# Sixteen input row tiles placed k times 32 bytes behind multiples of 512 bytes, in a kernel with three matmuls per weight block

## The chip, the cores and the metric

The kernel runs on one core of one Trainium2 chip. The metric is the device time of one execution in microseconds (us); the time before is the median of three runs. Profiled times count from the start of the span. PE is the matrix engine (TensorE), PEld its weight loads, ACT the scalar engine, DVE the vector engine, POOL GpSimd and SP the engine whose queue issues nearly all transfers.

## What is computed

The reference is a stack of layers over one sequence of 256 tokens of width 2048, in float32: a mixer (stick-breaking attention beside a gated delta rule), cross attention to a memory of 256 rows, a convolutional feed-forward layer of inner width 5632, an attention with forget gates and one with a sliding window. Nearly all of the work is in products of the activations with 11 weight matrices:

```python
proj = h @ w_in[l]                                   # 2048 x 7184
x = x + mixed @ w_out[l]                             # 2048 x 2048
x = x + memory_cross_attention(rmsnorm(x, xattn_norm[l]), mem_n, w_xq[l], w_xkv[l], w_xo[l])
u = causal_dwconv(h @ w_up, conv_w) + conv_b         # 2048 x 11264
x = x + (jax.nn.silu(gate) * up) @ w_down            # 5632 x 2048
p = h @ fox_w_in[j];  x = x + y @ w_out              # 2048 x 8224, 2048 x 2048
p = h @ swa_w_in[j];  x = x + y @ w_out              # 2048 x 4608, 2048 x 2048
```

## The kernel before

**Data.** Activations lie transposed: XT has 16 row tiles of 128 features by 256 tokens. A row tile that goes into a product is split into two parts that add up to it (`split`, L207): a rounded part in float32r, written by ACT, and the remainder, written by DVE. Both lie in one tile of 2 x 256 elements (2048 bytes in each partition): `xh` for the 16 scaled row tiles of the residual stream (pool `xp`, 16 buffers, made by `new_x` and `fox_x`), and `mv`, `mix` and `mm` for inner activations, in pools of their own. `xh` is written anew in five places (before w_in, w_xq, w_up, the forget-gate layer, the sliding-window layer), each time for k = 0 to 15 in order, so that row tile k always has buffer k.

**Weights.** Weights come from HBM in granules of up to KG = 8 row blocks of 128 x 256 (`granules`, L239): 1 MB each, in `wt`, NWT = 3 buffers. The first product of the kernel begins with smaller granules. Each granule is turned into float32r in chunks of up to KC = 4 row blocks: ACT copies the chunk to `wh` (L258), DVE subtracts it from `wt` to give the remainder `wl` (L259, listed as L147). `wh` and `wl` have NWC = 4 buffers each, of 4096 bytes in a partition. After each chunk `tick` lets the side work (attention heads, norms) go on by a step.

**Matmuls.** For each row block and each half of 128 columns, `linB` issues three matmuls of 128 x 256 into one accumulation: `wh` times the rounded part, `wh` times the remainder, `wl` times the rounded part. The weight block is the stationary operand, and each matmul loads it anew. `linA` swaps the roles: the row tile is stationary and the weights move. All are issued by `mm`, which is why the profile shows them under L136.

**Addresses.** In the built program `wh` and `wl` buffers begin 384 bytes behind a multiple of 512, and so does every block in them, since blocks are 512 or 1024 bytes apart. The `xh` tiles begin at 384 too, the `mv`, `mix` and `mm` tiles at 128.

**Order.** A scheduler orders the instructions of each engine by the dependences of tiles and by when buffers come free; each queue then runs its instructions in that order. A `wt` buffer is free again when DVE has made the last `wl` of its granule; that is what an SP transfer of weights waits for.

Of the kernel before, what the change touches and what calls it, by code (L numbers as in the profile page):

```python
# [10 lines left out]
F32R = mybir.dt.float32r  # L11
# [4 lines left out]

S, D, P = 256, 2048, 128
KT = D // P
KG, KC = 8, 4
NWT, NWC = 3, 4  # L20

WIDTH = {"norm": 1, "mem": 1, "gdn": 1, "sb": 1, "xa": 2, "at": 2}
NEG = -1e30
# [99 lines left out]
def body(ctx: ExitStack, tc: tile.TileContext, d: dict, out: bass.AP, stop=None):  # L123
# [6 lines left out]
    xp = Lined(ctx.enter_context(tc.tile_pool(name="xp", bufs=16)))  # L130
# [38 lines left out]
    def V(name):  # L169
        o, n = COLS[name]  # L170
        return cols[:, o : o + n]
# [35 lines left out]
    def split(mv, src, scale=None):  # L207

        if scale is None:
            act(mv[:, 0, :], src, AF.Copy)  # L210
            tt(mv[:, 1, :], src, mv[:, 0, :].bitcast(F32), ALU.subtract)
        else:
            act(mv[:, 0, :], src, AF.Copy, scale=scale)  # L213
            stt(mv[:, 1, :], src, scale, mv[:, 0, :].bitcast(F32), ALU.mult, ALU.subtract)
# [129 lines left out]
    def column(r):  # L344
# [10 lines left out]
        later("norm", work())  # L355
        return c

    def new_x(k, g):
        mv = xp.tile([P, 2, 256], F32R, tag="xh", name="xh")
        split(mv, XT[:, k, :], V(g)[:, k : k + 1])  # L360
        return mv

# [13 lines left out]
    def then(norm, g):  # L376
        xs = []

        def after(k):
            xs.append(new_x(k, g))  # L380
            norm.add(XT[:, k, :])

        return xs, after
# [27 lines left out]
    def first_x(k):  # L411
        n = 2 if k < 4 else 4
        if k % n == 0 and k not in made:
            src = d["xT"][k * P : (k + n) * P, :].rearrange("(k p) s -> p k s", p=P)
            nc.sync.dma_start(XT[:, k : k + n, :], src)
        if k not in made:
            made[k] = new_x(k, "mix_norm")
        return made[k]

    xh = [lambda k=k: first_x(k) for k in range(KT)]  # L420
# [343 lines left out]
    xh, after = then(norm, "xattn_norm")  # L764
# [10 lines left out]
    def new_mv():  # L775
        return mvbox[0].tile([P, 2, 256], F32R, tag="mv", name="mv")
# [25 lines left out]
    with tc.tile_pool(name="xa", bufs=2) as xa_:  # L802
# [61 lines left out]
        xh, after = then(norm, "ffn_norm")  # L864
# [15 lines left out]
    fx = []  # L880

    def fox_x(k):
        mv = xp.tile([P, 2, 256], F32R, tag="xh", name="xh")
        split(mv, XT[:, k, :], fg[:, k : k + 1])
        fx.append(mv)
        norm.add(XT[:, k, :])
        norm2.add(XT[:, k, :], V("final_norm")[:, k : k + 1])

    cw, cb = V("ffn_conv"), V("ffn_conv_bias")
    with tc.tile_pool(name="ff", bufs=2) as ff_:  # L890
# [15 lines left out]
        for n in range(22):  # L906
# [6 lines left out]
            for j in range(2):  # L913
                mv = new_mv()
# [9 lines left out]
    xh = fx  # L924
# [176 lines left out]
    for gidx in range(8):  # L1101
        c0 = 256 * gidx
        q = ap_.tile([P, 2, 256], F32, tag="qk", name="q")
        k = ap_.tile([P, 2, 256], F32, tag="qk", name="k")
# [24 lines left out]
    xh, after = then(norm, "norm_g_2b")  # L1129
# [103 lines left out]
def build(arrays, stop=None):  # L1233
    import concourse.bacc as bacc

    nc = bacc.Bacc("TRN2", target_bir_lowering=False, num_devices=1)
    d = {n: nc.dram_tensor(f"in_{n}", a.shape, F32, kind="ExternalInput").ap() for n, a in arrays.items()}
    out = nc.dram_tensor("out_0", (D, S), F32, kind="ExternalOutput").ap()
    with tile.TileContext(nc) as tc:
        body(tc, d, out, stop)  # L1240
    return nc
# [9 lines left out]
```

## Time and profile before

| | before |
|---|---|
| median of 3 runs | 2270.25 us (2270.0 to 2272.79) |
| the profiled execution | 2270.89 us |
| its span, first to last instruction | 2269.1 us |
| PE busy in the span | 2248.3 us (99%) |
| PEld busy | 2208.0 us (97%) |
| DVE, ACT, POOL busy | 1500.1, 1203.9, 119.0 us |
| matmuls that read an `xh` tile | 11,904 of 19,214 |
| moved from HBM | 375.66 MB, 166 GB/s over the span |

Between the span and the time of the same execution lie 1.8 us. Matmuls are pipelined: one that is listed with 283 ns overlaps the two behind it, so the distance from start to start is what counts, not the duration.

### The profile page before, as it was taken

To read this page: it belongs to the slowest core of one execution; us is meant where nothing else is said; L and a number is where in the kernel's file an instruction comes from. 1 tells how busy PE (TensorE), PEld (TensorE's weight loads), DVE (VectorE), ACT (ScalarE), POOL (GpSimd) and SP (SyncE) were. 2 spreads that over 40 slices of the span, in tenths; PEclk is the share of its full clock that TensorE was granted. 3 is DMA by queue.
4 is the path that set the end of the run, shared out by engine and by line. 5 is a ranking of instruction groups with operands and counts; after the bars stand their busy time and mean duration, and the time that the engine had idled before them with its cause. 6 is when DMAs were issued, how large, how long until landed. Compare 5 with 4: busy or idle time off the path is not lost.

```text
span 2269.1 us, 45530 instructions
## 1 busy us (share of the span) xinstructions
PE 2248.3 (99%) x19214; PEld 2208.0 (97%) x19214; DVE 1500.1 (66%) x2474; ACT 1203.9 (53%) x2036; POOL 119.0 (5%) x161
## 2 busy tenths in 40 slices
PE   9999999999999999999999999999999999999997
PEld 9999999999999999999999999999999999999997
DVE  7756566467587756656765777766666666787864
ACT  6544545356565534544544556555555554566652
POOL 1101010000000000000000000000110000000011
PEclk9999999999999999999999999999999999999999
DMA  7433434345455565555556546444444455444443
GB/s 265 149 131 131 147 118 146 112 160 196 164 189 184 168 202 185 167 186 191 185 167 204 181 164 214 151 168 167 168 166 168 149 186 186 152 165 149 159 159 111
DMA packets 62350, 380.69 MB, mean 168 GB/s; under 512 B 6593, under 2 KB 12865, under 8 KB 19521
## 3 DMA queue, kind: packets, MB, share of 16 engines
q1 hardware_dynamic: 60768, 375.94, 49.4%
q8 instruction: 150, 2.46, 0.4%
q10 hardware_dynamic: 1232, 1.06, 0.1%
q0 software_dynamic: 144, 0.79, 0.1%
q14 instruction: 56, 0.45, 0.1%
HBM read 375.66 MB, written 2.10 MB: 166 GB/s over the span
## 4 chain that ended last, share of the span: by engine, by line
PE 94%; DVE 3%; ACT 2%; issue 1%; POOL 0%; DMA 0%; SPq 0%; DVEq 0%; ACTq 0%; POOLq 0%
PE linb L136 79%; PE lina L136 7%; PE zps L136 2%; PE yps L136 1%; PE ptps L976 1%; PE nps L136 1%; DVE wl L147 1%; PE wsp L136 1%; PE xps L136 1%; DVE y L150 0%; ACT wh L258 0%; PE snp L136 0%; PE mps L136 0%; POOL e L492 0%; DMA wt<-in_w_in 0%
## 5 line engine op out<-in xcount | busy, mean ns | idle before, releaser
L136 PE MATMUL linb<-xh,wh 128*128 128x256 f32 x7104 | 1300.7, 285 | 2.2 <-ACT xh L213 1.7
L258 ACT ACTIVATE wh<-wt 128x1024 fp32r<-128x1024 f32 (+2 forms) x713 | 744.8, 1047 | 890.4 <-PE linb L136 738.7
L147 DVE TENSOR_TENSOR wl<-wt,wh 128x1024 fp32r<-128x1024 f32 (+2 forms) x713 | 869.8, 1223 | 467.3 <-ACT wh L258 461.0
L136 PEld LDWEIGHTS linb<-xh,wh 128*128 128x128 f32 x7104 | 1108.4, 192 | 10.8 <-issue 4.7
L136 PE MATMUL linb<-xh,wl 128*128 128x256 f32 x3552 | 1005.9, 283 | 0.0
L136 PEld LDWEIGHTS linb<-xh,wl 128*128 128x128 f32 x3552 | 681.6, 192 | 0.1
L136 PE MATMUL linb<-mv,wh 128*128 128x256 f32 x2560 | 462.6, 283 | 0.0
L136 PEld LDWEIGHTS linb<-mv,wh 128*128 128x128 f32 x2560 | 399.3, 192 | 0.5 <-issue 0.3
L136 PE MATMUL linb<-mv,wl 128*128 128x256 f32 x1280 | 362.3, 283 | 0.0
L136 PEld LDWEIGHTS linb<-mv,wl 128*128 128x128 f32 x1280 | 245.5, 192 | 0.2 <-issue 0.2
L136 PE MATMUL lina<-wh,xh 128*128 128x256 f32 x832 | 157.9, 286 | 0.0
L136 PEld LDWEIGHTS lina<-wh,xh 128*128 128x128 f32 x832 | 132.0, 192 | 0.6 <-issue 0.3
L136 PE MATMUL lina<-wl,xh 128*128 128x256 f32 x416 | 117.9, 283 | 1.0 <-DVE wl L147 1.0
L150 DVE SCALAR_TENSOR_TENSOR y<-pre,cols,y 128x256 f32<-128x256 f32 x248 | 103.4, 480 | 0.3 <-ACT y L504 0.2
L136 PE MATMUL linb<-mix,wh 128*128 128x256 f32 x512 | 94.1, 285 | 0.2
L136 PEld LDWEIGHTS linb<-mix,wh 128*128 128x128 f32 x512 | 80.0, 192 | 1.2 <-issue 0.3
L136 PEld LDWEIGHTS lina<-wl,xh 128*128 128x128 f32 x416 | 79.7, 192 | 1.2 <-DVE wl L147 1.2
L136 PE MATMUL linb<-mix,wl 128*128 128x256 f32 x256 | 72.7, 284 | 0.3 <-DVE wl L147 0.3
L147 DVE TENSOR_TENSOR pre<-linb,rstd 128x512 f32<-128x512 f32 x56 | 38.7, 692 | 41.3 <-PE linb L136 41.2
L1028 POOL CAST kd<-kd 64x512 fp32r<-64x512 f32 x32 | 36.2, 1131 | 355.2 <-ACT kd L1025 353.8
L150 DVE SCALAR_TENSOR_TENSOR XT<-linb,XT 128x512 f32<-128x512 f32 x48 | 33.2, 692 | 29.1 <-PE linb L136 29.0
L895 POOL MEMSET pre<- 128x4 f32 x44 | 4.3, 102 | 879.0 <-ACT wh L258 673.6
(291 smaller groups left out, 1800.5 us busy)
## 6 DMA issues: line engine op xcount, KB each, us to landing
wt<-in_w_up SPq DMA_DIRECT2D x88, 1024.0 KB, 5.2
wt<-in_fox_w_in SPq DMA_DIRECT2D x64, 1024.0 KB, 5.1
wt<-in_w_in SPq DMA_DIRECT2D x53, 1024.0 KB, 5.1
wt<-in_swa_w_in SPq DMA_DIRECT2D x36, 1024.0 KB, 5.1
wt<-in_w_down SPq DMA_DIRECT2D x32, 1024.0 KB, 4.9
wt<-in_w_out SPq DMA_DIRECT2D x16, 1024.0 KB, 5.3
wt<-in_fox_w_out SPq DMA_DIRECT2D x16, 1024.0 KB, 5.1
wt<-in_swa_w_out SPq DMA_DIRECT2D x16, 1024.0 KB, 5.2
```

The source lines that it names most:

```text
L136: nc.tensor.matmul(o, lhsT, rhs, start=start, stop=stop, skip_group_check=True)
L147: vec.tensor_tensor(o, a, b, op=op)
L150: vec.scalar_tensor_tensor(o, a, s, b, op0=op0, op1=op1)
L258: act(wh[:], wt[:, h : h + n, :], AF.Copy)
L895: gps.memset(pre[:, :, 0:2], 0.0)
L976: nc.tensor.transpose(tps[:, b * P : b * P + P], p[:, b * P : b * P + P], ident)
L1028: gps.tensor_copy(st[e][other, i], st[e][own, i])
```

## The change

Three edits. A row tile `xh` gets a buffer of 640 elements (2560 bytes, five times 512) of which 512 are used, beginning at element 8k, that is 32k bytes behind the buffer's start, for row tile k. Granules are halved: KG goes from 8 to 4 row blocks (512 KB), so that a granule is one chunk. `wt` gets NWT = 4 buffers of 4096 bytes in place of 3 of 8192.

```diff
-KG, KC = 8, 4
-NWT, NWC = 3, 4
+KG, KC = 4, 4
+NWT, NWC = 4, 4
...
+    def x_tile(k):
+
+        t = xp.tile([P, 640], F32R, tag="xh", name="xh")
+        return t[:, 8 * k : 8 * k + 512].rearrange("p (a b) -> p a b", a=2)
+
     def new_x(k, g):
-        mv = xp.tile([P, 2, 256], F32R, tag="xh", name="xh")
+        mv = x_tile(k)
         split(mv, XT[:, k, :], V(g)[:, k : k + 1])
         return mv
...
     def fox_x(k):
-        mv = xp.tile([P, 2, 256], F32R, tag="xh", name="xh")
+        mv = x_tile(k)
         split(mv, XT[:, k, :], fg[:, k : k + 1])
```

In the built program `wh` and `wl` stay at 384 bytes behind a multiple of 512, `mv`, `mix` and `mm` at 128, and `xh` tile k goes to 384 + 32k. So tile 0 keeps its place against the weights, tile 8 comes to 256 bytes from it, which is the place that `mv` has, and the 14 others come to places that no operand had. The pool `xp` grows by 16 times 512 bytes in a partition, and `wt` shrinks by as much (24 KB to 16 KB).

PE's instructions stand in the same order as before, and their number is the same. What moves is SP's queue. At its head it reads so before (`wt` are granules, 128x2048 is 1 MB; XT is the input, cols, twt, cst and braw are small constants):

```order
L415 DMA XT<-in_xT 128x4x256
L252 DMA wt<-in_w_in 128x1024 x2
L252 DMA wt<-in_w_in 128x2048
L530 DMA cols<-in_cols 128x641
L291 DMA twt<-in_w_gates 128x512
L252 DMA wt<-in_w_in 128x2048
L536 DMA cst<-in_consts 128x1248
L252 DMA wt<-in_w_in 128x2048
L186 DMA braw<-in_consts_b 128x160
L252 DMA wt<-in_w_in 128x2048 x50
```

and so now:

```order
L420 DMA XT<-in_xT 128x4x256
L252 DMA wt<-in_w_in 128x1024 x4
L535 DMA cols<-in_cols 128x641
L291 DMA twt<-in_w_gates 128x512
L252 DMA wt<-in_w_in 128x1024 x4
L541 DMA cst<-in_consts 128x1248
L186 DMA braw<-in_consts_b 128x160
L252 DMA wt<-in_w_in 128x1024 x100
```

Each granule of 1 MB became two of 512 KB; cst stands behind 2 MB of the third product's weights instead of behind 1 MB (line numbers from the second half of the file on are higher by 5).

The second place is ACT's queue at the end of the first product, where it makes the weights that PE waits for (`wh`), the squares of the first norm (`sq`) and its square root (rstd, rst). Before:

```order
L319 ACTIVATE sq<-XT 128x256 x2
L258 ACTIVATE wh<-wt 128x1024 x3
L201 ACTIVATE rstd<-rsa 128x256
L258 ACTIVATE wh<-wt 128x1024
L202 ACTIVATE rstd<-rstd 128x256
L203 ACTIVATE rst<-rstd 128x256
L258 ACTIVATE wh<-wt 128x1024
```

and now:

```order
L319 ACTIVATE sq<-XT 128x256 x3
L258 ACTIVATE wh<-wt 128x1024
L319 ACTIVATE sq<-XT 128x256 x2
L258 ACTIVATE wh<-wt 128x1024 x3
L201 ACTIVATE rstd<-rsa 128x256
L202 ACTIVATE rstd<-rstd 128x256
L203 ACTIVATE rst<-rstd 128x256
L258 ACTIVATE wh<-wt 128x1024
```

One chunk of weights moved ahead of two squares, and one moved behind the norm's square root.

## Rows read from the trace of the kernel before

**Rows 1.** The page, part 1: busy us (share of span) xinstructions.

```profile
PE 2248.3 (99%) x19214; PEld 2208.0 (97%) x19214; DVE 1500.1 (66%) x2474; ACT 1203.9 (53%) x2036; POOL 119.0 (5%) x161
```

**Rows 2.** The page, part 4: the chain that ended last, by line.

```profile
PE linb L136 79%; PE lina L136 7%; PE zps L136 2%; PE yps L136 1%; PE ptps L976 1%; PE nps L136 1%; DVE wl L147 1%; PE wsp L136 1%; PE xps L136 1%; DVE y L150 0%; ACT wh L258 0%; PE snp L136 0%; PE mps L136 0%; POOL e L492 0%; DMA wt<-in_w_in 0%
```

**Rows 3.** The page, part 5: groups, xcount | busy us, mean ns | idle before.

```profile
L136 PE MATMUL linb<-xh,wh 128*128 128x256 f32 x7104 | 1300.7, 285 | 2.2 <-ACT xh L213 1.7
L136 PE MATMUL linb<-xh,wl 128*128 128x256 f32 x3552 | 1005.9, 283 | 0.0
...
L136 PE MATMUL lina<-wh,xh 128*128 128x256 f32 x832 | 157.9, 286 | 0.0
...
L136 PE MATMUL lina<-wl,xh 128*128 128x256 f32 x416 | 117.9, 283 | 1.0 <-DVE wl L147 1.0
```

**Rows 4.** Windows, xh instructions only, feed-forward layer: PE, PEld busy, clock, DMA share, GB/s.

```profile
849.60:964.70 115.10, 115.10 (x960) 115.09 (x960) 0.00 (x0) 0.00 (x0) 1.00 0.54 178
```

**Rows 5.** Windows, mv instructions only, same layer, the product before that.

```profile
786.20:849.50 63.30, 63.30 (x528) 63.29 (x528) 0.75 (x2) 0.73 (x2) 1.00 0.58 193
```

**Rows 6.** Timeline in the stretch of rows 4: start, duration, engine, operation.

```profile
900.30 1.22 DVE L147 TENSOR_TENSOR wl<-wt,wh 128x1024 fp32r<-128x1024 f32 x1
...
900.42 0.73 ACT L210 ACTIVATE mv<-y 128x256 fp32r<-128x256 f32 x2 [0.73 <-DVE y L147]
900.53 0.28 PE L136 MATMUL linb<-xh,wl 128*128 128x256 f32 x1
900.54 0.31 PEld L136 LDWEIGHTS linb<-xh,wh 128*128 128x128 f32 x2
...
900.89 0.28 PE L136 MATMUL linb<-xh,wl 128*128 128x256 f32 x1
```

**Rows 7.** Timeline of PE right behind a break by side work.

```profile
1508.18 0.29 PE L136 MATMUL linb<-xh,wl 128*128 128x256 f32 x1
...
1508.53 0.28 PE L136 MATMUL linb<-xh,wl 128*128 128x256 f32 x1
```

**Rows 8.** Timeline of PE: four transposes; three score matmuls and what follows.

```profile
64.25 0.60 PE L560 MATMUL kps<-cst,KQ 128*128 128x128 f32 x4
...
1500.45 0.52 PE L136 MATMUL zps<-kd,qs 128*128 128x256 f32 x3
1500.82 0.34 PE L136 MATMUL zps<-cs,bset 96*128 96x384 bf16 x1
```

**Rows 9.** One tile, kps: duration ns min/median/max.

```profile
L560 PE MATMUL kps<-cst,KQ x16: 272/272/273, 64.2 to 369.8; 128*128 128x128 f32 x16
```

**Rows 10.** Groups by form on DVE: readers of pre, and writers of xh.

```profile
L150 DVE SCALAR_TENSOR_TENSOR y<-pre,cols,y 128x256 f32<-128x256 f32 x248 | 103.4, 480 | 0.3 <-ACT y L504 0.2
...
L150 DVE SCALAR_TENSOR_TENSOR xh<-XT,cols,xh 128x256 fp32r<-128x256 f32 x64 | 29.5, 480 | 0.4 <-ACT xh L213 0.4
```

**Rows 11.** Waits: who waited for whom, us in total, times, longest.

```profile
ACT wh L258 <- PE linb L136: 738.7, 457, 3.1
...
ACT wh L258 <- DMA wt<-in_w_in: 11.1, 5, 3.2
...
SPq L252 <- DVE wl L147: 1855.6, 339, 18.6
...
PE lina L136 <- DVE wl L147: 1.0, 1, 1.0
```

**Rows 12.** DMA issues, KB each, median us to landing; then one tile, wt: chunks, issues, landing.

```profile
wt<-in_w_xo SPq DMA_DIRECT2D x8, 512.0 KB, 3.6
...
L258 ACT ACTIVATE wh<-wt x713: 614/1060/1067, 3.9 to 2243.5; 128x1024 fp32r<-128x1024 f32 x170, 128x768 fp32r<-128x768 f32 x8, 128x512 fp32r<-128x512 f32 x1
L147 DVE TENSOR_TENSOR wl<-wt,wh x713: 692/1225/2325, 4.6 to 2244.5; 128x1024 fp32r<-128x1024 f32 x170, 128x768 fp32r<-128x768 f32 x8, 128x512 fp32r<-128x512 f32 x1
L252 SPq DMA_DIRECT2D wt<-in_w_up x88: 327/328/328, 632.7 to 1318.6; - x88
...
DMA to landing us min/median/max: 2.9/5.1/8.8
```

## The prediction

> **What bounds the kernel now.** I read the page's busy times first, then the chain of waits, then the steps of PE inside one stage. PE is busy for 99% of the span and its weight loads for 97% [rows 1], and the chain that ended last runs for 79% + 7% through the two helpers that multiply by weights [rows 2]. So a change counts if it shortens or lengthens PE's own steps, or if it makes PE wait.
>
> The step comes from windows. In a stretch of the feed-forward layer in which every matmul reads an `xh` tile, 960 of them take 115.10 us [rows 4], 119.9 ns each; the timeline of that stretch shows the same in small: from one `wl` matmul to the next, three steps later, 900.53 to 900.89 us, 0.36 us [rows 6]. At 120 ns the 11,904 matmuls that read `xh` (7104 + 3552 + 832 + 416) [rows 3] are 1428 us, 63% of the span. Each step holds one weight load and one matmul, and the next load starts when the running matmul does (900.54 beside 900.53) [rows 6]: PE reads a weight block and a row tile from SBUF at the same time, on which an argument for placement could rest.
>
> **The change, part by part.**
>
> *The place of the row tiles, as PE reads them.* Nothing is added to PE's queue and nothing is moved in it; what can change is the length of 11,904 steps. Two of the sixteen places are in the trace already. Tile 0 keeps its distance of 0 from the weights, the case of [rows 4]. Tile 8 goes to a distance of 256 bytes, which is where `mv` lies: 528 of its matmuls took 63.30 us, 119.9 ns each [rows 5]. Between these two places the difference is nothing that the rows can show, so 2 x 744 of the matmuls cost 0. The other 14 tiles, 14/16 of 11,904 = 10,416 matmuls, go to distances that no row has, so I bound them.
>
> Below, one step is at least what a weight load needs when little else is to be done: four transposes, each with a load of 128 columns, last 0.60 us [rows 8], of which the last is 0.272 [rows 9], so three steps are 0.328 and one is 109 ns. Steps of that length would save 11 ns on each of 10,416, 115 us. A nearer bound is the matmul stream itself: right behind a break three steps last 0.35 us, 1508.18 to 1508.53 [rows 7], 117 ns each, before the 120 ns set in. So 120 is not the least that this pair of streams can do; 3 ns on 10,416 is 31 us.
>
> Above, the nearest row is a matmul that reads its columns as two pieces: the score matmuls, whose third takes two runs of 128 columns. Three steps from 1500.45 to 1500.82 us are 0.37 us [rows 8], 123 ns each: 3 ns on 10,416 would cost 31 us the other way.
>
> I take 0, between these. The row that decides is the pair [rows 4] and [rows 5], the only one in which place alone differs, and it shows no difference at half the period of 512 bytes. A second reason holds for any arrangement of SBUF that repeats after 512 bytes or a half, a quarter or less of that: while a load goes through 512 bytes, the matmul goes through 1024 in about the same time, so the two addresses shift against each other by one whole period, or by several, in each matmul. Wherever the tile begins, the matmul passes the load's address equally often. A third: the stretch of [rows 6] has ACT and DVE writing SBUF in the middle of it, and the steps around are 0.12 us as elsewhere, so PE's reads don't show traffic of others.
>
> The Trainium skill speaks against this zero. In "TensorE: Matmul & The Clock Gate", sections "Back-to-back issue gap" and "LDWEIGHTS (loading the stationary operand)", 256 columns need 256/2.4 + 2.5 = 109 ns at the full clock, and a weight load of 128 columns 128/1.2 = 107 ns. By that page neither stream needs 120 ns, and 11 ns in each step would be something that a placement might remove; by its 109 ns the sum would be an estimated 2270 - 115 = 2155 us. The trace has the 109 ns for loads [rows 8], and 120 ns wherever both streams run [rows 4, 5].
>
> *The place of the row tiles, as ACT and DVE write them.* They write 5 x 16 tiles; DVE's half of 64 of these is listed with 480 ns each. Accesses off a round address are in the trace too: the convolutions read `pre` at offsets of 4 to 12 bytes, and DVE's instructions for it last 480 ns as well [rows 10]. So nothing that shows on DVE, and I take the same for ACT; if each of the 160 lasted 10 ns longer, it would be 1.6 us, most of it beside PE.
>
> *Halved granules, four buffers.* The work on a chunk stays: 713 `wh`, 713 `wl` [rows 12]. Each chunk now comes by a transfer of its own, where before one transfer brought up to two; so SP issues at most 713/2 = 357 more at 0.33 us [rows 12], 118 us of its time. What hides it is that SP waits for DVE's `wl` for 1855.6 us [rows 11]; nothing but more weights stands behind it, save the constants and the memory's rows.
>
> Supply: a buffer is now one chunk, four chunks in a circle against six. PE uses a chunk in 24 steps, 2.88 us, so a buffer must come back within 4 x 2.88 = 11.5 us. It needs a transfer, a copy and a subtraction: 3.6 us for 512 KB (the `w_xo` row) + 1.06 + 1.23 = 5.9 us [rows 12], and behind it stand up to four finished chunks in `wh` and `wl`. That ACT waits for PE to free a `wh` for 738.7 us and for a transfer only 11.1 [rows 11] says that the supply is ahead. Cost: 0. If the cover were gone, each late microsecond per chunk would be 713 us.
>
> What can be gained there is small: PE's longest entry of waiting for `wl` is 1.0 us in all [rows 11], and smaller transfers land earlier. At the head of SP's queue cst comes one granule later; its first use is far behind it. ACT's squares come behind one chunk, 1.06 us [rows 12]. I allow -2 to +3 us.
>
> **Sum.** 2270.89 us of the profiled execution + 0 (place) + 0 (granules) = 2271; that execution is 0.6 us above the median of 2270.25, so I give 2270. A difference under 0.2%, 4.5 us, is about what a measurement of this kernel cannot tell from no change.
>
> **The rivals.**
>
> *A shorter step.* If the 120 ns come from the load and the matmul starting in the same place of SBUF, other distances may let both run on. For: 117 ns right behind a break and 109 ns for loads alone [rows 7 to 9]. Against: 256 bytes of distance change nothing. At 117 ns, 2270 - 31 = 2239 us; at 109, 2155. Beside it stands the page named above, whose 109 ns is the lower of the two.
>
> *A longer step, the slower side.* Reads that begin off a round address may need one more access per row of columns, for the moving tile in `linB` and for the stationary one in `linA`. It decides as soon as the addition is more than the slack that PE's read has inside 120 ns, which is at most the 11 ns of the bound above. For: no PE operand in the trace begins at 32 or 64 bytes. Against: DVE pays nothing for it [rows 10]. At the 123 ns of the score matmuls, 2270 + 31 = 2301 us; with half the places affected, 2286.
>
> *Supply gives out.* A landing over 11.5 - 2.3 = 9.2 us, for chunk after chunk, makes PE wait; the longest landing now is 8.8 and the median 5.1 at twice the size [rows 12]. At 0.1 us per chunk it would be 2341 us.
>
> **How the numbers follow.** No change of the step 0.53: 2268 to 2273. Shorter step 0.24: 2155 to 2265, the nearer end likelier. Longer step 0.20: 2275 to 2330. Supply 0.03. Hence faster 0.25 (with 0.01 for granules that gain more than I allow), same 0.52, slower 0.23. For 8 in 10 the range takes the first case whole, some 0.14 of the shorter step down to 2238, and some 0.14 of the longer up to 2302. The first case's own range is 2268 to 2273.
>
> **What the profile after would show.** Right: windows in which only `xh` is read give 119.9 ns as before, tile by tile, and the DMA rows show 512 KB with about 3.6 us. A shorter or longer step shows in the same windows, in `xh` alone, with `mv` windows as before; its size times 10,416 must give the whole difference. If supply is it, PE's waits for `wl` or `wh` rise from 1.0 us to the size of the loss, and ACT's waits for transfers above 11.1. Wrong would be a time off by more than 4.5 us with all steps at 120 ns.

## The result, and the profile after

The changed kernel takes 2250.97 us (median of 3 runs, 2249.55 to 2251.7), 19.3 us less than the 2270.25 before: the ratio is 0.991, with a 95% interval of 0.989 to 0.993. That lies inside the range of the prediction and outside its likeliest case: 2268 to 2273 does not hold it. It is the rival with the shorter step, in the part of it near no change.

The page of the kernel after, its parts 1, 5 and 6 (in part 5: busy us, mean ns of one, idle before), answers to [rows 1, 3, 12]:

```profile
PE 2224.8 (99%) x19214; PEld 2183.3 (97%) x19214; DVE 1499.9 (67%) x2474; ACT 1203.6 (54%) x2036; POOL 119.3 (5%) x161
...
L136 PE MATMUL linb<-xh,wh 128*128 128x256 f32 x7104 | 1279.1, 283 | 3.3 <-ACT xh L213 1.9
...
L136 PE MATMUL linb<-xh,wl 128*128 128x256 f32 x3552 | 995.5, 280 | 1.4 <-DVE wl L147 1.4
...
L136 PE MATMUL linb<-mv,wh 128*128 128x256 f32 x2560 | 462.6, 283 | 0.0
...
wt<-in_w_up SPq DMA_DIRECT2D x176, 512.0 KB, 4.4
```

The same 19,214 matmuls keep PE busy for 23.5 us less, and DVE and ACT as long as before. Every group that reads `xh` takes less time; the group that reads `mv` does not (462.6 us, as before; its steps are in the windows below). The transfers are twice as many, half as large, and land sooner (`w_up`: 4.4 us in the median, 5.2 before), and SP's queue is no part of the loss or gain above 3 us (first experiment below).

Two windows of the kernel after, the first with `xh` instructions only in the stretch of [rows 4], the second with `mv` instructions only as in [rows 5] (us, then busy us and count of PE, PEld, DVE, ACT, granted clock, DMA share, GB/s):

```profile
850.00:940.00 90.00, 90.00 (x766) 90.00 (x765) 0.00 (x0) 0.00 (x0) 1.00 0.61 187
...
785.00:825.00 40.00, 40.00 (x336) 40.00 (x335) 0.75 (x2) 0.73 (x2) 1.00 0.60 186
```

A matmul on `xh` comes every 90.00/766 = 117.5 ns by count, 117.8 by start times, where it was 119.9. On `mv` it is 40.00/336 = 119.0 by count; the start times give 119.97, as before (at both ends of a window a matmul that overlaps it is counted too). The granted clock is 1.00 in both, which is also what [rows 4, 5] show, so this is not a matter of the clock.

The timeline of PE in that stretch (start, duration) shows the step in small, against the 0.36 us of [rows 6]:

```profile
902.70 0.28 PE L136 MATMUL linb<-xh,wl 128*128 128x256 f32 x1
...
903.05 0.28 PE L136 MATMUL linb<-xh,wl 128*128 128x256 f32 x1
...
903.40 0.28 PE L136 MATMUL linb<-xh,wl 128*128 128x256 f32 x1
...
903.75 0.29 PE L136 MATMUL linb<-xh,wl 128*128 128x256 f32 x1
```

From here on **distance** means the address of the moving operand minus that of the stationary one, in bytes within a partition, and **step** the mean time from one matmul's start to the next one's, taken from all start times of the trace below 145 ns apart and counted to the matmul that begins it. By distance, the steps of `linB` on `xh` in the kernel after are:

| distance | 0 | 32 | 64 | 96 | 128 | 160 | 192 | 224 |
|---|---|---|---|---|---|---|---|---|
| step, ns | 118.6 | 118.6 | 118.5 | 118.65 | 117.9 | 118.6 | 114.8 | 117.6 |
| distance | 256 | 288 | 320 | 352 | 384 | 416 | 448 | 480 |
| step, ns | 118.4 | 118.6 | 118.4 | 118.7 | 117.8 | 118.6 | 114.7 | 117.6 |

The second row of steps repeats the first to within 0.3 ns: what counts is the distance modulo 256. The mean of all is 117.9. Over the 11,520 steps from one `xh` matmul to the next that are below 145 ns in both traces, 1381.5 us became 1358.5: 22.9 us less. Between the two profiled executions lie 21.3 us, between the medians 19.3; most of the difference is what the granules cost, below. (One place is not measured alone here: each tile has only six steps in a row before its neighbour comes. What a place is worth by itself the next runs show.)

### The profile page after: what moved, and what is told of

It reads as the page before. It is cut to its first block, busy times and chain, and to the rows that moved or that the text cites. A ratio compares the mean times of both kernels' runs of the same rounds, so it can differ in the third digit from the quotient of the medians.

```text
span 2247.8 us, 46458 instructions
## 1 busy us (share of the span) xinstructions
PE 2224.8 (99%) x19214; PEld 2183.3 (97%) x19214; DVE 1499.9 (67%) x2474; ACT 1203.6 (54%) x2036; POOL 119.3 (5%) x161
## 4 chain that ended last, share of the span: by engine, by line
PE 93%; DVE 3%; ACT 2%; issue 1%; DMA 1%; POOL 0%; SPq 0%; DVEq 0%; ACTq 0%
PE linb L136 78%; PE lina L136 7%; PE zps L136 2%; PE yps L136 1%; PE ptps L981 1%; DVE wl L147 1%; PE nps L136 1%; PE wsp L136 1%; PE xps L136 1%; ACT wh L258 0%; PE snp L136 0%; PE mps L136 0%; DVE y L150 0%; DMA wt<-in_w_in 0%; DVE XT L150 0%
## 5 line engine op out<-in xcount | busy, mean ns | idle before, releaser
L136 PE MATMUL linb<-xh,wh 128*128 128x256 f32 x7104 | 1279.1, 283 | 3.3 <-ACT xh L213 1.9
L136 PEld LDWEIGHTS linb<-xh,wh 128*128 128x128 f32 x7104 | 1088.1, 188 | 12.5 <-issue 4.1
L136 PE MATMUL linb<-xh,wl 128*128 128x256 f32 x3552 | 995.5, 280 | 1.4 <-DVE wl L147 1.4
L136 PEld LDWEIGHTS linb<-xh,wl 128*128 128x128 f32 x3552 | 668.1, 188 | 1.7 <-DVE wl L147 1.6
L136 PE MATMUL linb<-mv,wh 128*128 128x256 f32 x2560 | 462.6, 283 | 0.0
L136 PE MATMUL lina<-wl,xh 128*128 128x256 f32 x416 | 117.0, 281 | 1.4 <-DVE wl L147 1.4
```

The lines of the kernel that those rows point to most:

```text
L136: nc.tensor.matmul(o, lhsT, rhs, start=start, stop=stop, skip_group_check=True)
```

## The experiments

Each result is compared with runs of the kernel before on the same chip, whose median lay between 2270.1 and 2270.5 us.

### The granules alone

```diff
+        t = xp.tile([P, 640], F32R, tag="xh", name="xh")
+        return t[:, 0:512].rearrange("p (a b) -> p a b", a=2)
```

This is the kernel after with every row tile at the start of its buffer, so at distance 0 as before.

> Half of the change alone: granules of 512 KB and four buffers, every xh tile at distance 0 from the weights. Theory 'place': the time is that of before, 2270 us (2268 to 2273), and windows with xh alone give 120 ns per matmul. Rival 'granules': the gain came with the smaller transfers, so the time is that of the changed kernel, 2251 us, with shorter steps although nothing moved in SBUF.

Measured: 2273.06 us (10 runs, 2271.15 to 2274.59), ratio 1.001 (1.0001 to 1.002). The halved granules cost 2.5 us, and the step on `xh` is 119.92 ns again (window with `xh` alone, 88.12/735):

```profile
850.00:940.00 90.00, 88.12 (x735) 88.23 (x736) 0.00 (x0) 0.00 (x0) 1.00 0.60 184
```

So the whole gain of the change, 2273.06 - 2250.97 = 22.1 us, is the placement, close to the 22.9 us that the steps gave. Where the granules cost time can be seen too. SP's timeline in the kernel after, where the second layer part begins:

```profile
540.07 2.45 SPq L791 DMA_DIRECT2D MT<-in_memT  x4
542.62 2.23 SPq L252 DMA_DIRECT2D wt<-in_w_xq  x1
```

The memory's rows, four transfers, now have a granule of `w_xq` directly ahead of them (at 539.47 us) and one directly behind, and they land 7.6 us after their issue in the median, where it was 5.6. That their neighbours in the queue slow them is likely and not shown. ACT waits for them, 0.22 us in the kernel before and 2.29 us in the kernel after:

```profile
549.48 0.51 ACT L213 ACTIVATE mm<-MT,cols 128x256 fp32r<-128x256 f32 x1 [0.22 <-DMA MT<-in_memT]
```

```profile
546.21 0.51 ACT L213 ACTIVATE mm<-MT,cols 128x256 fp32r<-128x256 f32 x1 [2.29 <-DMA MT<-in_memT]
...
554.22 1.04 ACT L258 ACTIVATE wh<-wt 128x1024 fp32r<-128x1024 f32 x1
```

Between these two lines ACT works without a break, on ten row tiles of the memory and a norm, so the granule behind this `wh` is not what came late; the memory's rows are. PE then waits for that `wh`. Its timeline in the kernel after, with the idle time in brackets:

```profile
555.32 0.51 PE L136 MATMUL linb<-xh,wh 128*128 128x256 f32 x2 [0.68 <-ACT wh L258]
557.20 0.39 PE L136 MATMUL linb<-xh,wl 128*128 128x256 f32 x1 [1.38 <-DVE wl L147]
```

These are 2.1 us. The kernel with the granules alone has the same two waits (0.62 and 1.39 us), and behind them a stretch with less than the full granted clock on average. The window 560 to 566 us of the kernel with the granules alone, and then of the kernel before:

```profile
560.00:566.00 6.00, 4.93 (x28) 4.93 (x29) 6.00 (x11) 6.00 (x13) 0.00 (x0) 0.72 0.43 128
```

```profile
560.00:566.00 6.00, 6.00 (x52) 5.98 (x51) 6.00 (x13) 6.00 (x12) 0.00 (x0) 1.00 0.52 176
```

For 3.4 us of these six, from 561.1 us on, the granted clock is half, the lower of its two levels, 1.2 GHz; PE does 28 matmuls in the six where it did 52. Waits and slow stretch together put PE 3.95 us back against the kernel before. The execution as a whole was only 3.0 us longer, as PE had come out of the first 62 us of the kernel 1.6 us ahead; the kernel with everything moved (below), which has the granules of before, came out of them 1.7 us ahead, so that part is not the granules' doing.

### All row tiles at one place: 192 and 32

```diff
-        return t[:, 8 * k : 8 * k + 512].rearrange("p (a b) -> p a b", a=2)
+        return t[:, 48:560].rearrange("p (a b) -> p a b", a=2)
```

for 192 bytes, and the same with `t[:, 8:520]` for 32.

> The changed kernel with one distance, 192 bytes, for all 16 row tiles. In the changed kernel the tiles at 192 and 448 bytes took 114.8 ns per matmul, all others 117.6 to 118.7. Theory 'each distance has its own step': 10,656 matmuls of linB save 5.2 ns each, 1248 of linA some 2.4 ns: 2270 - 58 = 2212 us. Rival 'it is the change of distance from one tile to the next that breaks the rhythm of 120 ns': with one distance the steps go back to 120 ns and the time to 2270 us.

> The changed kernel with one distance, 32 bytes, for all row tiles. Theory 'each distance has its own step': 118.6 ns as its tiles had in the changed kernel, 2270 - 11,904 x 1.4 ns = 2253 us. Rival 'change of distance': 120 ns and 2270 us.

Measured: 2226.45 us (2223.13 to 2226.82), ratio 0.980 (0.979 to 0.982), with all tiles at 192; 2245.49 us (2244.25 to 2247.43), ratio 0.989 (0.988 to 0.991), with all at 32. The sign was right and 192 is the better place, but at 192 the gain of 44 us fell short of the 58 that the steps of tiles 6 and 14 promised, and at 32 it was 25 us where 17 were expected. Two windows of that one execution, both with `xh` alone and every tile at 192, say why the first fell short:

```profile
690.00:760.00 70.00, 70.00 (x596) 70.00 (x596) 0.00 (x0) 0.00 (x0) 1.00 0.61 188
845.00:925.00 80.00, 80.00 (x708) 80.00 (x707) 0.00 (x0) 0.00 (x0) 1.00 0.60 195
```

The first has 117.4 ns in each step, the second 113.0, in the same layer, from the same code, at the same granted clock and nearly the same DMA share. At distance 192 PE has two rhythms that keep themselves up, 113.3 and 117.8 ns by start times, each for stretches of a hundred microseconds and more. At 32 the mean step is 117.2, not the 118.6 that its tiles had in the kernel after, and there too it is a mean of two levels. Two windows with all tiles at 32:

```profile
690.00:760.00 70.00, 70.00 (x602) 70.00 (x602) 0.00 (x0) 0.00 (x0) 1.00 0.60 188
850.00:930.00 80.00, 80.00 (x682) 80.00 (x681) 0.00 (x0) 0.00 (x0) 1.00 0.60 187
```

By start times these are 116.7 and 117.8 ns. So two rhythms are not a thing of 192 alone; what is special there is how short the shorter one is.

### Is the place 256 bytes on the same place?

```diff
+        return t[:, 64 * (k % 2) : 64 * (k % 2) + 512].rearrange("p (a b) -> p a b", a=2)
```

The rows 4 and 5 of the prediction had 0 and 256 alone, each by itself; here they take turns.

> The changed kernel with distances 0 and 256 bytes by turns, tile by tile. Theory 'each distance has its own step, and they repeat after 256 bytes': 120 ns for both, 2270 us. Rival 'change of distance': each tile breaks the rhythm of the one before, some 118.6 ns per matmul and 2253 us.

Measured: 2273.36 us (10 runs), ratio 1.0014 (1.0004 to 1.0023), the granules alone within 0.3 us. The steps are 119.9 ns at 0 and 119.97 at 256. Taking turns does nothing; so tiles 0 and 8 had 118.5 in the kernel after because their neighbours stood elsewhere.

### Distance or address?

Both kernels are the kernel before, with its granules, and one unused tile of 192 bytes: ahead of the pool of row tiles, which moves `xh`, `mv`, `mix` and `mm` by 192 against the weights, or ahead of the weights' pool, which moves all of them together.

```diff
+    pad = ctx.enter_context(tc.tile_pool(name="pad", bufs=1))
+    pad.tile([P, 48], F32, name="pad")
```

> The kernel before (granules of 1 MB, three buffers) with one unused tile of 192 bytes ahead of the pool of the row tiles. It shifts everything behind the weights: xh comes to a distance of 192 bytes, mv, mix and mm to 448, which is 192 again after 256. Theory 'distance': linB's 15,456 matmuls go from 119.9 to the 115.0 ns that the run with 192 bytes for xh alone showed, linA's 1440 to 117.6: 2270.5 - 76 - 3 = 2191 us. Rival 'only xh matters, or 448 is not like 192': some 2214 us. Rival 'it takes the small granules as well': 2270 us.

> The kernel before with the same unused tile of 192 bytes, but ahead of the weights' pool, so that weights and row tiles shift together and every distance stays as before. Theory 'distance': 120 ns and 2270 us. Rival 'the address of the row tiles themselves counts': the same gain as with the tile behind the weights, 2191 us.

Measured, all moved together: 2270.15 us (10 runs), ratio 0.9999 (0.9989 to 1.0008), window as in the kernel before:

```profile
850.00:940.00 90.00, 90.00 (x752) 90.00 (x751) 0.00 (x0) 0.00 (x0) 1.00 0.55 184
```

A shift of all addresses by 192 bytes changes nothing, so it is not the address as such that counts. Row tiles moved against the weights: 2220.58 us, ratio 0.979 (0.977 to 0.981), with a wide spread, 2192.67 to 2228.75, at a mean granted clock of 0.996 or 0.997 in all five. The execution profiled is the fastest of the five, 77 us below the kernel before and the only one near the 2191 us expected, and its `xh` window and timeline hold the short rhythm (82.28/726 = 113.3 ns; 0.34 us for three steps):

```profile
850.00:940.00 90.00, 82.28 (x726) 82.08 (x725) 0.00 (x0) 0.00 (x0) 1.00 0.55 184
```

```profile
900.04 0.28 PE L138 MATMUL linb<-xh,wl 128*128 128x256 f32 x1
...
900.38 0.28 PE L138 MATMUL linb<-xh,wl 128*128 128x256 f32 x1
...
900.72 0.28 PE L138 MATMUL linb<-xh,wl 128*128 128x256 f32 x1
```

Here the inner activations gain as well, as they stand at 448, which is 192 again: `mv` steps are 114.5 ns, `mix` 113.5.

### One place for each of the five stages

```diff
+PLACE = (176, 240, 208, 184, 200)
...
+        o = PLACE[made_at[0]] // 4
+        if k == KT - 1:
+            made_at[0] += 1
+        return t[:, o : o + 512].rearrange("p (a b) -> p a b", a=2)
```

The five numbers are the distances in `linB` before w_in, w_xq, w_up, the forget-gate layer and the sliding-window layer; the second kernel has 64, 160, 128, 16, 96.

> The changed kernel with one distance for all row tiles of a stage: 176 bytes for w_in, 240 for w_xq, 208 for w_up, 184 for the forget-gate layer, 200 for the sliding window. It reads the step in ns by distance around 192, which gave 113 to 114 ns in long stretches. Theory 'the optimum is a range of places': steps near 114 ns from 176 to 208, nearer 118 at 240. Rival 'only multiples of 64 or 32 bytes do': 176, 184, 200 and 208 are all near 118.

> The changed kernel with one distance per stage: 64 bytes for w_in, 160 for w_xq, 128 for w_up, 16 for the forget-gate layer, 96 for the sliding window. The theory that only multiples of 32 give a gain, and 192 alone the short rhythm: 64, 96, 128 and 160 at 117.5 to 118.7 ns as the mixed tiles had, 16 near 119.5 as 176 and 208 had: some 2252 us. Rival 'a distance held for a whole stage falls into a rhythm of its own': steps off these values by over 1 ns.

Measured, one execution each: 2269.7 and 2254.09 us. The steps by distance, each held through a whole stage:

| distance | 16 | 64 | 96 | 128 | 160 | 176 | 184 | 200 | 208 | 240 |
|---|---|---|---|---|---|---|---|---|---|---|
| step, ns | 117.4 | 117.2 | 119.9 | 118.7 | 117.7 | 119.2 | 120.05 | 120.1 | 119.2 | 117.2 |

My picture of a range of good distances around 192 fell: 8 bytes to either side of it the step is 120. The guess for 16 bytes fell as well (119.5 expected, 117.4 found), and 96 is at 119.9 where the mixed places of the kernel after gave 118.65. So the table of the kernel after is not one of the places' own worth: a tile's steps also carry what its neighbours left. These here are means too: at 64 the step changes between 117.0 and 117.8 from stretch to stretch.

### The products with swapped roles

In `linA` the row tile is stationary, so that a row tile at 192 gives the distance -192, which is 64 modulo 256. Here `linA`'s weights go 128 bytes further, which makes it 192 (`wh` and `wl` get 64 elements more for it), and the row tiles lie at 192 by the unused tile. Granules are those of the change.

```diff
-        for wh, wl, i, mv, first, last in granules(w, runs, c0):
+        for wh, wl, i, mv, first, last in granules(w, runs, c0, o=32):
```

> The changed kernel's granules, the unused tile of 192 bytes ahead of the row tiles, and linA's weights 128 bytes further back in their buffers, so that in linA, where the weights are the moving operand, the moving operand too lies 192 bytes (mod 256) behind the stationary one. Theory 'what counts is moving minus stationary address': linA's steps go from 117.6 to 115 ns, 1440 x 2.6 = 4 us less than with the tile alone, and the granules cost some 2.5 us: 2190 us. Rival 'linA has its own limit': 117.6 ns stay, and 2194 us.

Measured: 2221.45 us, ratio 0.976 (0.970 to 0.981), but three runs at 2220 to 2223 and one at 2195.93, where 2190 were expected. The step in `linA` fell from 117.5 to 114.4, so distance with its sign, moving minus stationary, is the right measure. The profiled execution is one of the three, and its feed-forward stage kept the long rhythm from end to end:

```profile
850.00:940.00 90.00, 90.00 (x766) 90.00 (x765) 0.00 (x0) 0.00 (x0) 1.00 0.61 187
```

This execution (2220.32 us) is 27.65 us longer than the profiled one of the kernel with the unused tile alone (2192.67 us), and the feed-forward layer accounts for nearly all of it: from its first `linB` matmul on `xh` to its last on `mv`, the same instructions took 746.2 us here and 719.1 us there.

### Pushing PE into the short rhythm

Row tile 0, or tiles 0 and 8, at 160 and all others at 192, in the kernel just above:

```diff
+        t = xp.tile([P, 576], F32R, tag="xh", name="xh")
+        o = 56 if k % 8 == 0 else 64
+        return t[:, o : o + 512].rearrange("p (a b) -> p a b", a=2)
```

(With tile 0 alone, `k == 0`.) The idea is that six steps at 160 bring PE to the first tile at 192 in another phase. No trace shows the phase itself, and the mean of these steps turned out near one of the rhythms (117.7 ns beside 117.8), so the runs show that it works and not why.

> As the run with the unused tile and linA's weights 128 bytes further back, but row tile 0 lies 160 bytes behind the weights, tiles 1 to 15 at 192 (mod 256). At 192 two rhythms were seen that each go on for hundreds of us, 113.3 and 117.8 ns, and in the changed kernel every tile at 192 that came after one at 160 went into 113.3. Theory 'tile 0 sets the rhythm': each product of 96 matmuls starts anew and runs at 113.3, the feed-forward layer too in every execution; 9990 matmuls near 114, 666 at 118.6, mv and mix near 114.5: some 2270 - 85 = 2185 us, and the executions within 6 us of each other. Rival 'the rhythm is chance': executions spread from 2190 to 2225 us as with the tile alone.

> As the run before, with tiles 0 and 8 at 160 bytes. Theory 'tile 0 sets the rhythm': a second start in each product costs 666 x 5 ns = 3 us where the rhythm was right and gains where side work had broken it: 2183 to 2188 us. Rival 'chance': a spread from 2190 to 2225 us.

Measured: 2204.09 us (2202.03 to 2205.77), ratio 0.971 (0.969 to 0.972), and 2199.6 us (2197.59 to 2201.17), ratio 0.969 (0.968 to 0.971). The spread has gone from 27 us to 4, and the feed-forward stage is in the short rhythm in both. First the window of the kernel with tile 0, then of that with two tiles, all instructions:

```profile
850.00:940.00 90.00, 90.00 (x794) 90.00 (x793) 67.09 (x94) 48.62 (x62) 0.92 (x9) 1.00 0.61 191
```

```profile
850.00:940.00 90.00, 90.00 (x791) 90.00 (x790) 66.34 (x90) 47.87 (x61) 0.82 (x8) 1.00 0.62 191
```

By start times, the tiles at 160 included, these are 113.7 and 114.1 ns. From the end of a tile at 160 on, the steps run 117, 120, 117, 116, 114 and then 113, 113, 114 on and on. The time with tile 0 alone missed what I expected by 19 us: the stages with attention stay at about 115 to 118, so the tile at 160 does not hold the short rhythm there. The kernel with two such tiles is the best of the study, 3.1% faster than before and 51 us faster than the change.

### Which of the three matmuls gains?

```diff
+        t = xp.tile([P, 640], F32R, tag="xh", name="xh")
+        return t[:, 0:608].rearrange("p (a b) -> p a b", a=2)[:, :, 0:256]
```

The rounded part stays at 0 and the remainder goes to 192, so that one matmul in three has the good distance.

> The small granules, each row tile's rounded part at distance 0 and its remainder at 192 bytes (mod 256) from the weights, so that one of the three matmuls of a weight block in linB has the short distance. Theory 'each matmul's step follows its own moving operand': about 120 + 120 + 113 ns, 117.7 on average, on 11,904 matmuls some 27 us below the run with small granules and distance 0: 2246 us. Rival 'the longest of the three sets the rhythm': 120 ns and 2273 us.

Measured: 2251.61 us (2249.93 to 2252.58), ratio 0.992 (0.990 to 0.994). That is 21.5 us below the granules alone, and about half of what 192 for all gives; 27 were expected. It isn't the one matmul that shortens: `wh` times rounded takes 118.3 ns, `wh` times remainder 118.3, `wl` times rounded 117.0. A step's length is not set by its own two addresses alone; the gain of the one better place is shared by all three steps.

## Why the prediction was right, and where it was not

The forecast of 2270 us and its mechanism, no change of the step, were wrong. The range held all the same, because it took in a part of the rival with the shorter step (chance 0.14); for the main line of the argument that is luck.

**What bounds the kernel** held: PE's share stayed at 99%, and 22.9 us of shorter steps came out as 22.1 us of time.

**The place, as PE reads it: taken as 0, measured -22.1 us.** This is the term that failed. On 10,416 steps, my own count, it is 2.1 ns in each; but tiles 0 and 8, which I had left out of that count, gained as well (118.6 and 118.4 ns in the table above). The bound of 3 ns from [rows 7] came near by luck, for I misread the row: its times are printed to 10 ns, and in the trace's nanoseconds the three steps are 358 ns, 119.3 each and not 117. The 123 ns from [rows 8], my price of a longer step, are 362/3 = 120.7 in the same way. The bound of 11 ns from the loads alone [rows 8] stayed out of reach (best 6.6, from 119.9 to 113.3). Its three reasons, one by one:

- *The pair [rows 4, 5].* The rows were read rightly, 0 and 256 are equal, and the kernel in which they take turns shows it again. What I drew from it was wrong: the pattern repeats after 256 bytes, so the two rows were one place measured twice. Two points that may be a period apart say nothing of what lies between.
- *The shift by a whole period.* I argued that the matmul passes the load's address equally often wherever it begins. Steps between 113 and 120 ns for different beginnings contradict it. That two self-sustaining rhythms exist at one distance suggests what the argument left out: that the phase between load and matmul is not given but settles. The phase itself is in no trace.
- *No trace of ACT and DVE in PE's steps.* This held, and was beside the point: what changed the step was the distance between PE's own two operands.

The Trainium skill, in "SBUF — State Buffer", section "Who interferes with whom", gives PE two independent read ports and says that PE never waits on anyone. That agrees with ACT's and DVE's traffic leaving no mark. It does not cover what is measured here: with nothing changed but the distance between PE's two operands, steps went from 119.9 to 113.3 ns. The 109 ns that the prediction took from the Trainium skill, "TensorE: Matmul & The Clock Gate", section "Back-to-back issue gap", is given there for an isolated matmul; of a stream of loads and matmuls the section says that both together set the spacing, which the prediction passed over. No run reached it with both streams on; the shortest rhythm is 113.3 ns.

**The place, as ACT and DVE write it: 0.** Right: DVE 1499.9 us against 1500.1, ACT 1203.6 against 1203.9 [rows 1].

**The granules: 0, with -2 to +3 allowed.** Measured +2.5, in the allowance, by a cause I had not seen. I named the constants and the memory's rows as what stands behind weights on SP, and did not ask what happens to them. They landed 2 us later, between two granules of `w_xq`; ACT, which has them ahead of the next `wh` in its queue, waited for them, and PE waited 2.1 us for ACT. Supply of weights in general did not give out.

**The rivals.** The shorter step, chance 0.24, is what happened, and its "against" (256 bytes change nothing) was the failing argument again. It named the mechanism as load and matmul starting in the same place; the distance of 0 is indeed a slow place at 119.9, but so are 96, 184 and 200, so "not in the same place" is not a sufficient description. A longer step appeared nowhere: 120.1 ns is the longest of all places tried.

**What was to be seen** was named rightly in part: the shorter step in `xh` windows alone, and `mv` as before. The difference is spread over all 11,904 steps, though, and not over 10,416.

What stays open is why 192 modulo 256, and what keeps each rhythm up. The trace shows when instructions start and not what SBUF or the sequencer does within one. That the wide spread of two kernels comes from the two rhythms is inferred from one profiled execution of each, one in the short and one in the long rhythm through the feed-forward layer, where 27.1 us of their difference lie, and from the spread going away with the tiles at 160; the other executions have no trace.

## What to carry to other kernels

Where each matmul loads a weight block anew and PE is the bound, the distance between the two operands in SBUF is worth a try of one line: here an unused tile of 192 bytes ahead of a pool gave 2%. A "no effect" read from two places counts for these two only, above all when both are multiples of the same power of two. And a step that settles into a rhythm must be measured over whole stages and several executions, since neighbours are part of it, and since one distance can have two rhythms. And a difference of 3 ns in a step must not be read from times printed to 10 ns.

## What the runs showed of the chip that was not expected

- The step of a load with a matmul of 128 x 256 in float32r depends on the moving minus the stationary address modulo 256: 119.9 ns at 0, 117.2 in the mean at 32 and 64, 118.7 at 128, 113.3 at best at 192, and 120.05 and 120.1 at 184 and 200.
- At 192 there are two rhythms, 113.3 and 117.8 ns, each stable for a hundred microseconds and more; at 32 there are two as well, 116.7 and 117.8. One kernel with 192 took from 2192.67 to 2228.75 us, and with two of sixteen tiles at 160, 2197.59 to 2201.17.
- Moving weights and row tiles together by 192 bytes changes nothing (ratio 0.9999).
- A wait of 2.1 us of PE can cost more than itself: behind it the granted clock was at half for 3.4 us in the kernel with the granules alone, and not in the profiled execution of the kernel after.
